# A hybrid decoder layer whose input projection is regrouped by one level of Strassen's algorithm in two passes

## The chip, the cores and the metric

The kernel runs on one core of one Trainium2 chip. A core has five engines that run at the same time, each with an instruction queue of its own that it works through strictly in order: TensorE (PE in the profile) multiplies matrices and writes its sums to PSUM, VectorE (DVE), ScalarE (ACT) and GpSimd (POOL) work element by element, and SyncE (SP) here only issues DMAs between DRAM and the on-chip memory SBUF. Engines wait for each other through semaphores. PEld in the profile is the loading of TensorE's stationary operand, which runs beside the products.

The metric is the device time of one execution in microseconds (us); lower is better. Three runs of the kernel before gave 1719.65, 1719.75 and 1719.79 us, a median of 1719.75 us.

## The reference, cut to what matters

One decoder layer over 1024 positions and 2048 channels, all in float32:

```python
proj = x @ w_in                       # [1024, 2048] @ [2048, 7176]
q, k, v, g_att, fg, c_b, c_c, c_h, g_conv, p_u, g_pool = split(proj)
# 8 heads of 128: softmax of q k / sqrt(128) plus the forget gates' cumulative logs, causal
y_att  = forgetting_attention(q, k, v, fg, b_f) * silu(g_att)
y_conv = c_b * causal_conv3(c_c * c_h) * silu(g_conv)
y_pool = pool_map(causal_means(p_u)) * pool_scale * silu(g_pool)
x = layer_norm(2 ** 0.25 * x + concat(y_att, y_conv, y_pool) @ w_out)
```

Leaving out the eight forget logits `fg`, `proj` has 7168 columns: 56 blocks of 128. Eight of them are `v`, eight each are `q`, `k` and `g_att`, and 24 belong to the convolution and the pooling.

## The kernel before

**Products.** [...] A matmul has a 128x128 stationary operand and up to 512 moving columns.

**Stages.** `x`, transposed, is loaded once (`load_x`), split, and kept on chip as 32 tiles of [128, 2, 512]. First come `v` and the forget logits, with positions on partitions: `x` is the stationary operand, and the weights move in chunks of 512, 260 and 260 columns (`V_CHUNKS`); the results go to `v_dram`. Then 48 blocks of 128 columns are projected in the transposed layout (`project`, `run_project`): the weights are stationary, and `x` moves in two halves of 512 positions. A block takes 16 (parts of the 2048 channels) x 2 (halves) x 3 = 96 matmuls. The last stage multiplies the gated branches `y`, which are reloaded from `y_dram`, with `w_out` and ends in the LayerNorm.

**What sets the order.** Weights come through a stream: `w_load` issues the DMA on SP, `w_split` splits, and `next_w` keeps two splits and two loads ahead. The work of a branch is written as a list of steps; `run_project` takes one step of `side` (gates, attention) and one of `pooling` after every 12 matmuls. The 24 steps of a head's attention (`attention_steps`) so run under the 288 matmuls of the next head's three blocks. A scheduler then orders each engine's queue at build time, by its own model of when an operand will be there; that order is fixed on the chip.

**Attention of a head.** `scores` computes a block of 128 keys by 512 queries and adds the gate term on DVE; `fold` keeps the running maximum on DVE. `across` and `to_all` bring the row values to all partitions by way of `m_dram`. `probs` adds them to the scores (DVE, line 392), takes the exponential (ACT), folds the sum (POOL, line 361) and splits the result (ACT, DVE). `values` multiplies with `v`, `finish` applies the gate and stores `y`. Pooling's window sums (`means`) run on POOL.

```python
def mm3(acc, wh, wl, xh, xl, start, stop):
    nc.tensor.matmul(acc, wh, xh, start=start, stop=False)
    nc.tensor.matmul(acc, wh, xl, start=False, stop=False)
    nc.tensor.matmul(acc, wl, xh, start=False, stop=stop)
```

Of the kernel before, what the change touches and what calls it, by code (L numbers as in the profile page):

```python
# [26 lines left out]
P = 128  # L27
# [6 lines left out]
V_CHUNKS = (512, 260, 260)  # L34
# [5 lines left out]
SLOTS = 46  # L40
WARM_UP = 8


@with_exitstack
def layer(ctx: ExitStack, tc: tile.TileContext, xt, x, wm, wv, b_f, conv_w, pool_w, pool_scale,
# [3 lines left out]
    sb = ctx.enter_context(tc.tile_pool(name="sb", bufs=1))  # L49
# [9 lines left out]
    # one float32 [128, 1024] row block  # L59
    def f4(name):  # L60
        return sb.tile([P, S], F32, tag="b", bufs=SLOTS, name=nm(name))

    # high and low part of a [128, 512] block
    def hl(name):
        return sb.tile([P, 2, H], F32R, tag="b", bufs=SLOTS, name=nm(name))

# [7 lines left out]
    def mm3(acc, wh, wl, xh, xl, start, stop):  # L74
        nc.tensor.matmul(acc, wh, xh, start=start, stop=False)  # L75
        nc.tensor.matmul(acc, wh, xl, start=False, stop=False)  # L76
        nc.tensor.matmul(acc, wl, xh, start=False, stop=stop)  # L77

    # ---- constants
# [15 lines left out]
    # the tensor engine's clock comes up while the first loads are under way  # L95
# [8 lines left out]
    v_dram = dr.tile([NST, P, D // 2], F32, tag="vd", name="v_dram")  # L104
    y_dram = dr.tile([KT, 2, P, H], F32, tag="yd", name="y_dram")
    c_dram = dr.tile([NH * NST, P], F32, tag="cd", name="c_dram")
    m_dram = dr.tile([NH * 4, H], F32, tag="md", name="m_dram")

    # ---- weights: a stream of [128, <=512] chunks, split as they arrive
# [3 lines left out]
    def w_load(src, cols):  # L113
        raw = sb.tile([P, 512], F32, tag="wr", bufs=4, name=nm("wr"))
        nc.sync.dma_start(raw[:, :cols], src)
        return raw, cols

    def w_split(raw, cols):
        hi = sb.tile([P, 512], F32R, tag="wh", bufs=3, name=nm("wh"))
        lo = sb.tile([P, 512], F32R, tag="wl", bufs=3, name=nm("wl"))  # L120
        split(hi[:, :cols], lo[:, :cols], raw[:, :cols])
        return hi, lo

    plan = deque()
    v0 = 0
    for w in V_CHUNKS:
        for k in range(KT):
            plan.append((wv[k, :, v0 : v0 + w], w))
        v0 += w
    n_mt = wm.shape[0]  # L130
    for m in range(n_mt):
        for kc in range(4):
            plan.append((wm[m, kc], 512))
# [14 lines left out]
    xs = [[hl("x"), hl("x")] for _ in range(KT)]  # L148
    fgz = const.tile([P, NST, NH], F32, tag="fgz", name="fgz")

    def load_x(k):
        raw = f4("xraw")
        for h in range(2):
            cuts = [0, 128, 512] if k == 0 and h == 0 else [0, 512]
            for c0, c1 in zip(cuts, cuts[1:]):
                cs = slice(h * H + c0, h * H + c1)
                nc.sync.dma_start(raw[:, cs], xt[k, :, cs])
                if k == 0 and h == 0 and c0 == 0:
                    fill()
                split(xs[k][h][:, 0, c0:c1], xs[k][h][:, 1, c0:c1], raw[:, cs])  # L160

    v0 = 0
    for c, w in enumerate(V_CHUNKS):
        banks = [bank("acc") for _ in range(4)] + [bank("aux") for _ in range(4)]
        for k in range(KT):
            if c == 0:
                load_x(k)
                if k == 2:
                    nc.sync.dma_start(bf_sb, b_f.partition_broadcast(P))
                    nc.sync.dma_start(cw_sb, conv_w)  # L170
                    nc.sync.dma_start(psc_sb, pool_scale)
            wh, wl = next_w()
            for st in range(NST):
                sl = slice(st % 4 * P, st % 4 * P + P)
                xk = xs[k][st // 4]
                mm3(banks[st][:, :w], xk[:, 0, sl], xk[:, 1, sl], wh[:, :w], wl[:, :w], k == 0, k == KT - 1)
        cols = min(w, D // 2 - v0)
        for st in range(NST):
            vf = f4("vf")
            if st % 2:  # L180
# [515 lines left out]
```

## Time and profile before

| what | value |
|---|---|
| runs (3) | 1719.65 to 1719.79 us, median 1719.75 |
| the profiled execution: its span | 1719.5 us |
| around the span, by the median of the runs | 0.25 us |
| VectorE, ScalarE, GpSimd busy in the whole span | 46%, 27%, 9% |
| weight chunks loaded for `proj`, transposed layout | 192 of 256 KB, 2.7 us to landing |
| mean DMA rate over the span | 91 GB/s |
| written to DRAM in the span | 19.50 MB |

The page gives no time of the profiled execution but its span, from the first to the last instruction. A share of busy time is an average over stages: VectorE's 46% hides that its tenths in the page's 40 slices run at 6 to 7 during attention and at 1 to 3 in the projections of pooling and convolution. The chain that ended last is followed back from the last instruction, and tells which engine's work could not be moved without moving the end.

### The profile page before, as it was taken

The page shows a single profiled execution, that of the slowest core. Times are in us where ns is not written, and L with a number is a line of the kernel's source. Part 1 is how long each engine was busy: PE and PEld are TensorE (multiplying, and loading weights), DVE is VectorE, ACT ScalarE, POOL GpSimd, SP SyncE. Part 2 cuts the span into 40 slices and gives each one's busy share as a digit, 9 for nine tenths or more (in the row PEclk, how much of TensorE's full clock was granted, in tenths as well). Part 3 has the DMA queues.
Part 4 walks back from the last instruction along what each step waited for, and adds up shares of the span by engine and source line. Part 5 has one row for each costly group of instructions (what it writes and reads, how often), then busy time and mean ns, then how long its engine had stood idle before and what let it go on. Part 6 is the DMA issues. An engine that isn't in the chain of part 4 may idle for free.

```text
span 1719.5 us, 20754 instructions
## 1 busy us (share of the span) xinstructions
PE 1698.1 (99%) x7965; PEld 1420.8 (83%) x7965; DVE 792.7 (46%) x1486; ACT 470.0 (27%) x857; POOL 154.3 (9%) x204
## 2 busy tenths in 40 slices
PE   9999999999999999999999999999999999999997
PEld 7899888888888888888878888888888888887686
DVE  4221326676767676766751212121213443365436
ACT  4211223342433333433421111111112332232210
POOL 0000000211212020202132230000000000000000
PEclk9999999999999999999999999999999999999999
DMA  6232322222222222212222121211112554355523
GB/s 223 90 114 75 88 61 60 82 68 82 66 74 68 82 73 68 92 54 89 68 76 63 56 61 49 62 49 50 47 47 65 185 188 140 120 171 178 173 69 101
DMA packets 95043, 155.94 MB, mean 91 GB/s; under 512 B 11168, under 2 KB 26592, under 8 KB 94944
## 3 DMA queue, kind: packets, MB, share of 16 engines
q1 hardware_dynamic: 94944, 154.62, 29.9%
q8 instruction: 62, 1.02, 0.3%
q14 instruction: 37, 0.30, 0.1%
HBM read 135.08 MB, written 19.50 MB: 90 GB/s over the span
## 4 chain that ended last, share of the span: by engine, by line
PE 89%; DMA 5%; DVE 3%; issue 1%; ACT 1%; POOL 1%; SPq 0%; DVEq 0%
PE acc L75 24%; PE acc L76 24%; PE acc L77 24%; PE aux L76 6%; PE aux L77 5%; PE aux L75 5%; DMA wr<-w_out 4%; DVE wl L72 1%; ACT wlast L71 1%; DMA m<-m_dram 0%; DVE r L595 0%; DVE pt L72 0%; DVE r L596 0%; DVE bst L565 0%; DVE t L392 0%
## 5 line engine op out<-in xcount | busy, mean ns | idle before, releaser
L75 PE MATMUL acc<-x,wh 128*128 128x512 f32 x1536 | 598.8, 390 | 0.0
L76 PE MATMUL acc<-x,wh 128*128 128x512 f32 x1536 | 598.1, 389 | 0.0
L77 PE MATMUL acc<-x,wl 128*128 128x512 f32 x1536 | 597.9, 389 | 0.0
L72 DVE TENSOR_TENSOR wl<-wr,wh 128x512 fp32r<-128x512 f32 (+1 forms) x352 | 243.4, 694 | 588.8 <-ACT wh L71 583.9
L71 ACT CAST wh<-wr 128x512 fp32r<-128x512 f32 (+1 forms) x352 | 210.2, 602 | 778.4 <-PE acc L76 524.4
L77 PEld LDWEIGHTS acc<-x,wl 128*128 128x128 f32 x1536 | 288.4, 188 | 60.9
L75 PEld LDWEIGHTS acc<-x,wh 128*128 128x128 f32 x1536 | 288.6, 188 | 57.7
L76 PEld LDWEIGHTS acc<-x,wh 128*128 128x128 f32 x1536 | 288.6, 188 | 57.3
L76 PE MATMUL acc<-wl,y 128*128 128x512 f32 x256 | 100.4, 392 | 2.5 <-DVE wl L72 2.3
L75 PE MATMUL acc<-wh,y 128*128 128x512 f32 x256 | 100.0, 390 | 0.1
L77 PE MATMUL acc<-wh,y 128*128 128x512 f32 x256 | 99.7, 390 | 0.0
L76 PE MATMUL aux<-wl,y 128*128 128x512 f32 x192 | 75.8, 395 | 2.3 <-DVE wl L72 2.3
L75 PE MATMUL aux<-wh,y 128*128 128x512 f32 x192 | 75.6, 394 | 1.9 <-ACT wh L71 1.9
L361 POOL TENSOR_TENSOR m<-m,t 128x256 f32<-128x256 f32 (+1 forms) x64 | 74.7, 1168 | 23.8 <-ACT t L393 19.9
L77 PE MATMUL aux<-wh,y 128*128 128x512 f32 x192 | 75.3, 392 | 0.0
L72 DVE TENSOR_TENSOR pt<-t,pt 128x512 fp32r<-128x512 f32 (+1 forms) x96 | 71.8, 763 | 4.5 <-ACT pt L71 2.9
L392 DVE TENSOR_TENSOR t<-t,m 128x512 f32<-128x512 f32 (+1 forms) x96 | 58.5, 658 | 25.6 <-DMA m<-m_dram 25.2
L71 ACT CAST pt<-t 128x512 fp32r<-128x512 f32 (+1 forms) x96 | 49.9, 530 | 73.7 <-DVE pt L72 61.6
L351 DVE SCALAR_TENSOR_TENSOR t<-aux,t 128x512 f32<-128x512 f32 (+1 forms) x96 | 52.5, 547 | 30.9 <-PE aux L77 29.8
L593 POOL TENSOR_TENSOR r<-r,gb 128x512 f32<-128x512 f32 x1 | 1.7, 1673 | 697.6 <-ACT r L592 697.6
L75 PE MATMUL acc<-wh,x 128*128 128x260 f32 (+1 forms) x192 | 61.3, 319 | 0.0
L76 PE MATMUL acc<-wl,x 128*128 128x260 f32 (+1 forms) x192 | 61.0, 318 | 0.1
(152 smaller groups left out, 1899.0 us busy)
## 6 DMA issues: line engine op xcount, KB each, us to landing
wr<-wm SPq DMA_DIRECT2D x192, 256.0 KB, 2.7
wr<-w_out SPq DMA_DIRECT2D x128, 256.0 KB, 3.4
m<-m_dram SPq DMA_DIRECT2D x32, 256.0 KB, 3.6
out<-r SPq DMA_DIRECT2D x32, 256.0 KB, 2.8
xraw<-xt SPq DMA_DIRECT2D x31, 256.0 KB, 4.3
xr<-x SPq DMA_DIRECT2D x31, 256.0 KB, 4.0
yraw<-y_dram SPq DMA_DIRECT2D x26, 256.0 KB, 3.7
y_dram<-gate SPq DMA_DIRECT2D x24, 256.0 KB, 2.0
```

Source lines behind the costliest of these rows:

```text
L71: nc.scalar.copy(hi, src)
L72: nc.vector.tensor_tensor(lo, src, hi.bitcast(F32), ALU.subtract)
L75: nc.tensor.matmul(acc, wh, xh, start=start, stop=False)
L76: nc.tensor.matmul(acc, wh, xl, start=False, stop=False)
L77: nc.tensor.matmul(acc, wl, xh, start=False, stop=stop)
L351: nc.vector.scalar_tensor_tensor(tj[:, c0:H], acc[:, c0:], SCALE, tj[:, c0:H], ALU.mult, ALU.add)
L361: eng.tensor_tensor(m[:, c0:H], prev[:, c0:H], t[n, j][:, c0:H], op)
L392: nc.vector.tensor_tensor(tj[:, c0:H], tj[:, c0:H], mx[n][:, H + c0 :], ALU.add)
L593: nc.gpsimd.tensor_tensor(r, r, gb[1][:, cs], ALU.mult)
```

## The change

**The algorithm.** Two 128-column blocks of `w_in` form a pair (28 pairs). For a pair, `proj` is a 2x2 block product: two halves of the positions by two halves of the channels on one side, two halves of the channels by two blocks of columns on the other. Strassen's algorithm (in Winograd's form) makes such a product from 7 block products instead of 8, by sums and differences of blocks taken before and after. A block product is 8 x 3 = 24 matmuls of 512 columns (`Pair.product`).

**Two passes.** The first pass goes over all pairs and does four products of each (`p1`, `p6`, `p5`, `p7`), with the operands `11`, `s1`, `s2`, `s3` of `x` (`s` are sums). POOL makes the three weight combinations (`mix`, `mix_last`) from four raw blocks of 512 KB, and DVE and ACT split them as [128, 1024] tiles (`operand`). Two partial results of 512 KB per pair and one weight combination go to DRAM (`a_dram`, `b_dram`, `t_dram`). The second pass does the other three products (`12`, `22`, `s4`) with weights from the stream, and adds each to its partial result, which is loaded back (`load_pair`, `second`). Attention, pooling and convolution run beside the second pass; `tick` takes a step after every third channel part, that is after 9 matmuls.

**Other parts.** `v` is a pair's block like the others, in the transposed layout, and is turned by 8 transposes of 128x128 per head on TensorE (`turn_v`). The forget logits take 64 matmuls of their own, with the 16 columns of high and low parts stationary (`gate_sums`). The addition in `probs` and two multiplications of the convolution are on POOL. All of `y` goes through DRAM. The on-chip tiles lie in three pools that follow one another (first pass; second pass; output projection), so that a pool's first tiles reuse memory of the pool before.

```diff
+    def load_22(k):
+        row, r22 = rows[k], half("x22", "xr")
+        nc.sync.dma_start(r22, xt[KH + k, :, H:])
+        s1 = row[:, H:]
+        nc.vector.tensor_tensor(s1, s1, r22, ALU.add)
+        nc.gpsimd.tensor_tensor(r22, s1, row[:, :H], ALU.subtract)
+        nc.sync.dma_start(s2_dram[k], r22)
+        keep_x("s2", k, r22)
+        keep_x("s1", k, s1)
...
+        def mix(self):
+            r = self.raw
+            self.t3 = f4("t3", "w1")
+            nc.gpsimd.tensor_tensor(self.t3, r[3], r[1], ALU.subtract)
+            nc.gpsimd.tensor_tensor(r[1], r[1], r[0], ALU.subtract)
+            nc.gpsimd.tensor_tensor(r[3], r[3], r[1], ALU.subtract)
+
+        def mix_last(self):
+            r = self.raw
+            nc.gpsimd.tensor_tensor(r[2], r[2], r[3], ALU.subtract)
+            nc.sync.dma_start(t_dram[self.p], r[2])
+
+        def product(self, acc, src, name, more=False):
+            wh, wl = operand(src)
+            for k in range(KH):
+                ws = slice(k * P, k * P + P)
+                x = xs[name, k]
+                mm3(acc, wh[:, ws], wl[:, ws], x[:, 0], x[:, 1], not more and k == 0, k == KH - 1,
+                    skip_group_check=more)
...
+        def p6(self):
+            self.b, self.u2 = bank("aux"), half("u2", "u2")
+            self.product(self.b, self.raw[3], "s2")
+            nc.vector.tensor_tensor(self.u2, self.b, self.ca[:, :H], ALU.add)
...
+    for p in pairs[2:-2]:
+        p.load(0, 1, 3, 2)
+        p.mix()
+        p.mix_last()
+        p.p1()
+        p.p6()
+        p.p5()
+        p.p7()
...
+    def second(p, j):
+        acc, name = bank("acc"), LATER[j][0]
+        for c in range(2):
+            wh, wl = next_w()
+            for i in range(4):
+                k = c * 4 + i
+                ws = slice(i * P, i * P + P)
+                x = xs[name, k]
+                mm3(acc, wh[:, ws], wl[:, ws], x[:, 0], x[:, 1], k == 0, k == KH - 1)
+                tick()
+        ca, cb = arrived[p]
+        dst = (ca[:, :H], ca[:, H:], cb[:, :H])[j]
+        nc.vector.tensor_tensor(dst, acc, dst, ALU.add)
...
+        def turn_v(n):
+            def go():
+                acc, th = bank("aux"), hl("v", "v")
+                for a in range(4):
+                    c = (n * 4 + a) * P
+                    nc.tensor.transpose(acc[:, a * P : a * P + P], vt[:, c : c + P], ident)
+                split(th[:, 0], th[:, 1], acc)
+                v[n] = th
+            return go
...
         def probs(n, j):
             def go():
                 tj, c0 = t[n, j], first(n, j)
                 cw = min(c0, 256)
-                nc.vector.tensor_tensor(tj[:, c0:H], tj[:, c0:H], mx[n][:, H + c0 :], ALU.add)
+                nc.gpsimd.tensor_tensor(tj[:, c0:H], tj[:, c0:H], mx[n][:, H + c0 :], ALU.add)
                 nc.scalar.activation(tj[:, c0:H], tj[:, c0:H], AF.Exp)
```

**How the order moves.** Three places matter to what follows. In the prints below a name's number only tells tiles apart.

POOL, the second half of the queries of one head's attention. Before, its only two-tensor work there was the running sum `m`:

```order
L370 MEMSET w_626_4376 32x32
L361 TENSOR_TENSOR m_3697<-t_3698 128x512
L361 TENSOR_TENSOR m_3697<-m_3697,t_3759 128x512 x2
L361 TENSOR_TENSOR m_3697<-m_3697,t_3814 128x512
L361 TENSOR_TENSOR m_3697<-m_3697,t_3814 128x384
L361 TENSOR_TENSOR m_3697<-m_3697,t_3884 128x256
```

The same place in the change (line 639 is the addition in `probs`, line 608 the sum):

```order
L639 TENSOR_TENSOR t_4863<-t_4863,m_4862 128x512 x2
L639 TENSOR_TENSOR t_4922<-t_4922,m_4862 128x512 x2
L639 TENSOR_TENSOR t_4972<-t_4972,m_4862 128x512
L639 TENSOR_TENSOR t_4972<-t_4972,m_4862 128x384
L639 TENSOR_TENSOR t_5056<-t_5056,m_4862 128x256
L639 TENSOR_TENSOR t_5056<-t_5056,m_4862 128x128
L608 TENSOR_TENSOR m_4862<-t_4863 128x512
L608 TENSOR_TENSOR m_4862<-m_4862,t_4922 128x512 x2
```

Eight additions now stand on POOL ahead of the eight folds, and the exponentials, splits and `values` products wait for them.

DVE, one pair of the first pass in the change (`wop` is the low part of a product's weights; `u`, `ca`, `cb` are results taken out of PSUM):

```order
L277 TENSOR_TENSOR u_131_822<-aux_821,ca_791 128x512
L110 TENSOR_TENSOR wop_932<-wb_915,wop_931 128x1024
L282 TENSOR_TENSOR cb_853<-acc_852,u_131_822 128x512
L110 TENSOR_TENSOR wop_963<-wb_919,wop_962 128x1024
L286 TENSOR_TENSOR ca_791<-aux_821,ca_791 128x512
L287 TENSOR_TENSOR cb_853<-acc_852,ca_791 128x512
L110 TENSOR_TENSOR wop_994<-wb_917,wop_993 128x1024
L110 TENSOR_TENSOR wop_1023<-t_144_923,wop_1022 128x1024
```

The splits of the next pair's weights (`wop_932` and on) have moved ahead of this pair's last evacuations, so that a product's operands stand ready a product early.

SP where the output projection begins. Before, the loads of `y` stand among the loads of `w_out`, the first four of them far earlier, and no store stands there:

```order
L115 DMA wr_10303<-w_out 128x512
L115 DMA wr_10343<-w_out 128x512
L286 DMA yraw_10297<-y_dram 128x512
L286 DMA yraw_10320<-y_dram 128x512
L115 DMA wr_10383<-w_out 128x512
```

In the change:

```order
L156 DMA wr_10359<-w_out 128x512
L156 DMA wr_10381<-w_out 128x512
L530 DMA y_dram<-pa_9828 128x512 x2
L538 DMA yraw_10282<-y_dram 128x512
L538 DMA yraw_10284<-y_dram 128x512
L538 DMA yraw_10286<-y_dram 128x512
```

The first load of `y` now stands behind the store of the last convolution block's `y`.

SP between the two passes of the change (there is no such place before); `ca` and `cb` are the last pairs' partial results:

```order
L291 DMA a_dram<-ca_4033 128x1024
L292 DMA b_dram<-cb_4237 128x1024
L482 DMA pa_4408<-a_dram 128x1024
L483 DMA pb_4409<-b_dram 128x1024
L482 DMA pa_4412<-a_dram 128x1024
L483 DMA pb_4413<-b_dram 128x1024
L156 DMA wr_4417<-wp 128x512
```

The second pass's first weights `wr` stand behind the last stores and four loads of 512 KB.

More of the change, by code (lines that the diff above doesn't have):

```diff
@@ L162, in layer @@
[L162 to L177, printed above, removed]
[L178 to L187 removed]
+    xs = {}
@@ new lines, in layer @@
+    last_pairs = pairs[-2:]
+    for p in last_pairs:
+        p.load(0, 1, 3, 2)
+        p.mix()
+        p.mix_last()
+    for p in last_pairs:
+        p.p1()
+    for k in range(KH):
+        load_12(k)
+    for p in last_pairs:
+        p.p6()
+    for k in range(KH):
+        load_22b(k)
+    for p in last_pairs:
+        p.p5()
+    for k in range(KH):
+        load_s4(k)
+    for p in last_pairs:
+        p.p7()
+    leave()
+    enter("stream", STREAM)
+    small = enter("second", SECOND)
@@ L453, in means @@
             src, d, i = u, 1, 0
-            sums = [f4("sum"), f4("sum")]
+            sums = [f4("sum", "pl"), f4("sum", "pl")]
             while d < w:
```

460 lines of the change are left out of this document (294 added, 166 removed).

## The prediction, made before the change was timed

> **What bounds the kernel now.** I read the page first, for the engine that is never idle and for the chain that ended last, then the windows of three stages.
>
> ```profile
> span 1719.5 us, 20754 instructions
> ...
> PE 1698.1 (99%) x7965; PEld 1420.8 (83%) x7965; DVE 792.7 (46%) x1486; ACT 470.0 (27%) x857; POOL 154.3 (9%) x204
> ...
> PEclk9999999999999999999999999999999999999999
> ...
> PE 89%; DMA 5%; DVE 3%; issue 1%; ACT 1%; POOL 1%; SPq 0%; DVEq 0%
> ```
>
> PE is busy 99% of the span at full granted clock, and 89% of the chain is PE. That busy figure counts overlapping matmuls, so I take the price of a matmul from windows in which nothing else ran on PE: first the 260-column products for `v`, then a head's attention with the next head's blocks, then the last blocks of the projection (columns: busy time of PE, PEld, DVE, ACT, POOL, granted clock, DMA share, GB/s).
>
> ```profile
> 110.00:190.00 80.00, 80.00 (x653) 79.00 (x653) 19.16 (x52) 15.35 (x38) 2.02 (x9) 1.00 0.30 84
> ...
> 398.80:477.70 78.90, 78.90 (x362) 65.84 (x362) 54.44 (x112) 29.97 (x57) 12.89 (x17) 1.00 0.25 74
> ...
> 1120.00:1300.00 180.00, 180.00 (x796) 149.10 (x795) 39.10 (x53) 26.57 (x45) 0.00 (x0) 1.00 0.18 49
> ```
>
> A 512-column matmul costs 180.00 / 796 = 0.226 us, a 260-column one 80.00 / 653 = 0.1225 us. PE sets the time in every stage but the first and the last microseconds, so a matmul taken away is time taken away, as long as nothing else becomes late.
>
> **Term 1, the products: -135 us.** Before, 48 blocks of 96 matmuls are 4608 x 0.2261 = 1042 us; `v` takes 16 x 8 x 3 = 384 matmuls of 512 columns (87 us) and 768 of 260 (94 us): 1223 us. After, 28 pairs x 7 products x 24 = 4704 matmuls are 1064 us, and the gate sums' 64 are 14.5 us. The transposes are new; the nearest row is the one transpose of the gates.
>
> ```profile
> 200.82 0.39 PE L77 MATMUL acc<-x,wl 128*128 128x512 f32 x1
> 201.05 0.27 PE L227 MATMUL aux<-ident,cum 128*64 128x128 f32 x1
> 201.07 0.47 PE L75 MATMUL acc<-x,wh 128*128 128x512 f32 x1
> 201.39 0.39 PE L76 MATMUL acc<-x,wh 128*128 128x512 f32 x1
> ```
>
> From 200.82 to 201.39 run two 512-column products and the transpose: 0.57 - 0.45 = 0.12 us for it. Its 0.27 us of duration would be the upper end. At 0.12 us, 64 for `v` and 16 small ones take 10 us. 1064 + 14.5 + 10 = 1088, so 135 us go; at 0.27 us it would be 123.
>
> The Trainium skill (TensorE: Matmul & The Clock Gate, Part 4: PE-mode transpose) gives about 275 ns for a 128x128 transpose inside a kernel; by that the 80 would take 22 us and the sum would end 12 us later. The row's spacing speaks for the smaller price, but for one transpose only.
>
> **The first pass in steady state: nothing.** A pair's 96 matmuls last 21.7 us. Beside them stand the following.
>
> ```profile
> L72 DVE TENSOR_TENSOR wl<-wr,wh 128x512 fp32r<-128x512 f32 x320 | 229.6, 720 | 511.6 <-ACT wh L71 506.8 <-PE acc L76 4.7
> ...
> L421 DVE TENSOR_TENSOR gate<-aux,gate 128x512 f32<-128x512 f32 x16 | 10.6, 659 | 0.0
> ...
> L463 POOL TENSOR_TENSOR sum<-sum,u 128x1024 f32<-128x1024 f32 x4 | 10.0, 2504 | 0.3
> ...
> 5.00:10.00 5.00, 4.83 (x20) 3.54 (x20) 2.79 (x5) 2.21 (x4) 0.00 (x0) 1.00 0.88 290
> ```
>
> POOL's four combinations take 4 x 2.5 = 10 us. DVE's four splits of 1024 columns (2 x 0.72 each) and four evacuations (0.66) take 8.4 us. Seven transfers of 512 KB are 3.7 MB, which at the 290 GB/s of the start are 12.7 us. All lie under 21.7 us, and the DVE rows of a pair show the next pair's splits ahead of this pair's evacuations. If that cover were gone, each us over 21.7 would cost 26 us, once per pair.
>
> **Term 2, the start: +22 us.** The first products now wait for 512 KB blocks, and by SP's order `p1` ends only when 7.1 MB have come: 7.1 MB / 290 GB/s + 3 = 27 us, while PE has 64 matmuls (14.5 us) for it. Then POOL is late: before the second half of `s2` it has 12 combinations of 2.5 us, four of them for the third pair, and 8 subtractions of 512 columns.
>
> ```profile
> 4.60 0.60 PE L75 MATMUL acc<-wh,x 128*128 128x512 f32 x1
> ...
> L361 POOL TENSOR_TENSOR m<-m,t 128x512 f32<-128x512 f32 x24 | 38.1, 1589 | 20.6 <-ACT t L393 19.9
> ...
> xraw<-xt SPq DMA_DIRECT2D x31, 256.0 KB, 4.3
> ```
>
> 12 x 2.5 + 8 x 1.59 = 43 us from about 13 us on (3.2 MB stand on SP up to the first pair's third block), and some 10 us (two such loads in a row) for `x` blocks whose buffers come free only after a store: 66 us. `p6`'s rest and two `p5` products follow (13 us), which makes 79 us for 224 matmuls (51 us): 28 us idle. Before, the first product starts at 4.6 us, and 20 matmuls instead of 22 in the window from 5 to 10 us show what little is lost later: about 6 us in all. The difference is 22. Bounds: +5 if DMA alone counts, +35 if POOL and loads never overlap.
>
> **Term 3, two handovers: +14 us.**
>
> ```profile
> wr<-wm SPq DMA_DIRECT2D x192, 256.0 KB, 2.7
> ...
> yraw<-y_dram SPq DMA_DIRECT2D x26, 256.0 KB, 3.7
> y_dram<-gate SPq DMA_DIRECT2D x24, 256.0 KB, 2.0
> ...
> cq<-c_dram SPq DMA_DIRECT2D x8, 512.0 KB, 4.0
> ```
>
> Between the passes SP holds the first `wr` loads behind the stores of the last results: two evacuations (1.3), a store of 512 KB (about 3, from 2.0 for half), the `pa` and `pb` loads and the weights (4.0), the cast (0.6): some 10 us, of which 16 gate products cover 3.6. At the output projection the first `y` load stands behind the last `y` store: evacuation and product (0.66 + 1.4), load (3.7), cast and split (1.3): 7 us. Together 14; bounds 6 (loads go ahead) and 24 (each waits for a full landing in turn).
>
> **Term 4, attention: +40 us.** Steps now come after 9 matmuls instead of 12, so PE would need 78.9 - 72 x 0.226 + 8 x 0.12 = 63.6 us per head. DVE's 54.4 us change by -12 additions in `probs`, +6 splits of 0.72, +9 accumulations of 0.66 and about 4 instructions of pooling or convolution of 0.72:
>
> ```profile
> L392 DVE TENSOR_TENSOR t<-t,m 128x512 f32<-128x512 f32 (+1 forms) x96 | 58.5, 658 | 25.6 <-DMA m<-m_dram 25.2
> ...
> L361 POOL TENSOR_TENSOR m<-m,t 128x256 f32<-128x256 f32 (+1 forms) x64 | 74.7, 1168 | 23.8 <-ACT t L393 19.9
> ```
>
> 54.4 - 7.9 + 4.3 + 5.9 + 2.9 = 59.6 us. POOL's 12.9 us grow by 12 x 1.17 and by 2.5 (convolution) to 9 (pooling): 29 to 36 us. And the two engines get in each other's way:
>
> ```profile
> 386.11 3.07 POOL L361 TENSOR_TENSOR m<-m,t 128x512 f32<-128x512 f32 x2 [0.33 <-ACT t L393]
> ...
> 386.25 1.78 DVE L72 TENSOR_TENSOR pt<-t,pt 128x512 fp32r<-128x512 f32 x1
> 387.95 1.77 DVE L72 TENSOR_TENSOR wl<-wr,wh 128x512 fp32r<-128x512 f32 x1
> 389.65 0.68 DVE L72 TENSOR_TENSOR pt<-t,pt 128x512 fp32r<-128x512 f32 x1
> ...
> 392.26 1.38 DVE L392 TENSOR_TENSOR t<-t,m 128x128 f32<-128x128 f32 x1
> ...
> 394.17 1.50 DVE L72 TENSOR_TENSOR pt<-t,pt 128x512 fp32r<-128x512 f32 x1
> ```
>
> A DVE subtraction takes 0.68 us alone and 1.78 beside a POOL fold. The four lengthened ones here lose about 4 us to 12.9 us of POOL work, 0.32 us per us; 16 to 23 us more of POOL work so add 5 to 7 us. DVE comes to 65 to 67 us per head against PE's 64: from 69% busy to full. I take 69 us per head, DVE's load and a few waits in order: +5 x 8 = +40. Bounds: 0, if every wait disappears under PE; +14 a head, if half of the 24.5 us that DVE sat idle in the window before stay.
>
> The Trainium skill (SBUF — State Buffer, Who interferes with whom) says that a DVE instruction with two SBUF inputs and a GpSimd instruction that reads SBUF exclude each other for a whole instruction. The rows agree (1.78 against 0.68 us), and it speaks against moving `probs`' addition to POOL: by it alone, with no overlap left between POOL's 33 us and DVE's 60, a head would take 93 us and the kernel 1856. The second rival below is this mechanism, priced by rows.
>
> **The sum.** The profiled execution's span is 1719.5 us, 0.25 under the median of the runs. 1719.5 - 135 + 22 + 14 + 40 = 1660.5, and 1661 us with what lies around it.
>
> **The rivals.**
> - PE stays the bound in attention too: term 4 is nothing, 1621 us. For it: DVE's waits for ACT in the page are waits for free buffers, not work that is late. Against it: 65 us of DVE in 64.
> - DVE and POOL set attention's pace: at 78 us a head, some +112, 1733 us. Place: `probs`' additions and folds in line on POOL, the weight splits behind them on DVE. It decides the sign from (135 - 36) / 8 = 12.4 us above 63.6, that is 76 us a head. For it: the lengthened rows. Against it: the exclusion took only 4 us per head so far.
> - The first pass is not bound by PE, since POOL, stores and loads wait for each other in SP's single queue: at 23.2 us a pair, +39, 1700 us. Against it: 12.7 us is the longest load beside 21.7. That fewer products are not had at all is ruled out by the order: 4704 matmuls stand there.
>
> **How the numbers follow.** The forecast, 1661 us, has a chance of 0.62; with the bounds of terms 2 and 3 and a head between 65 and 73 us it spans 1625 to 1700. PE bound throughout 0.20; DVE and POOL 0.12, three quarters of it slower; the first pass 0.06. The range is 1612 to 1722. About 0.2% is what a measurement of this kernel can tell from no change: faster by more than that 0.88, within it 0.03, slower 0.09.
>
> **What would show it.** Of the terms: the windows of the first pass should show 96 matmuls in 21.7 us per pair; PE should wait some 28 us in the first 80 us, for POOL's subtractions last; two gaps of 6 to 8 us should stand where the passes change; a head should take 66 to 73 us with DVE above 90%. The prediction is wrong if PE waits in the first pass, or if a head takes under 65 or over 74 us.

## The result and the profile after

The changed kernel takes 1832.4 us, the median of four runs (1830.65 to 1834.0); the kernel before took 1719.7 beside it. The ratio is 1.066 (95% interval 1.064 to 1.067): **slower by 112.7 us**, where 59 us less were forecast, and outside the range of 1612 to 1722.

The page of the changed kernel, in the same lines as before:

```profile
span 1831.5 us, 19913 instructions
...
PE 1645.2 (90%) x7053; PEld 1327.4 (72%) x7053; DVE 1081.2 (59%) x1643; ACT 581.9 (32%) x919; POOL 612.2 (33%) x436
...
PEclk7799999999999997989899989999998999999999
...
PE 55%; DVE 13%; DMA 12%; POOL 12%; issue 6%; ACT 2%; SPq 0%; DVEq 0%; POOLq 0%; ACTq 0%
```

PE has 912 instructions fewer and is no longer the whole of the chain: DVE, DMA and POOL hold 37% of it. The row of the clock is new: it was 9 in all 40 slices before. The two stages at the kernel's beginning are seen in the windows of both kernels (busy time of PE, PEld, DVE, ACT, POOL, granted clock, DMA share, GB/s), first after, then before:

```profile
0.00:100.00 100.00, 73.77 (x260) 51.69 (x261) 74.08 (x72) 34.34 (x51) 56.06 (x50) 0.80 0.61 216
100.00:600.00 500.00, 500.00 (x2207) 414.02 (x2206) 222.41 (x182) 108.47 (x115) 240.70 (x90) 1.00 0.46 160
600.00:720.00 120.00, 91.68 (x369) 69.55 (x368) 45.95 (x61) 30.00 (x46) 30.29 (x18) 0.87 0.59 203
```

```profile
0.00:100.00 100.00, 98.72 (x459) 82.43 (x460) 37.03 (x61) 34.96 (x60) 2.15 (x29) 1.00 0.52 165
```

From 100 to 600 us the first pass runs as forecast, 500 us for 2207 products, 0.2266 us each, at full clock and without a wait. At the start and around 680 us PE loses what it lost nowhere before. The third place is attention. The next two windows run from the first score product of head 0 to that of head 7, so they hold seven heads; before, then after:

```profile
252.88:805.40 552.52, 552.20 (x2521) 459.90 (x2520) 379.15 (x775) 208.59 (x390) 90.72 (x119) 1.00 0.25 74
```

```profile
745.10:1339.90 594.80, 500.09 (x2098) 398.86 (x2098) 446.60 (x824) 259.95 (x453) 239.40 (x238) 0.92 0.36 120
```

A head took 552.5 / 7 = 78.9 us with 360 products; it takes 594.8 / 7 = **85.0 us with 300**. DVE is busy for 63.8 us of it and POOL for 34.2: neither is full, and PE waits.

What each stage lost, from the spacing of PE's successive products in the timeline less what they take at full rate (0.2266 us per 512 columns), as the difference from the kernel before:

| stage | forecast, us | measured, us | of it at half clock |
|---|---|---|---|
| products fewer, by their count and the spacing measured | -135 | -135 | |
| start, 0 to 100 us | +22 | +42 | 9 |
| first pass in steady state | 0 | -2 | |
| handover between the passes, 600 to 720 us | +7 | +37 | 5 |
| attention, 720 to 1450 us | +40 | +171 | 42 |
| handover to the output projection and rest | +7 | +4 | -1 |

The sum is +117 beside a span that is 112 us longer; the 5 us between are small irregularities of spacing that I did not follow. The last column depends on where a gap is taken to end and a slow product to begin, and is good to about 10 us.

**What waits in attention.** From the list of waits of the changed kernel (who waited for whom, us in total, times, the longest):

```profile
ACT t L640 <- POOL t L639: 95.1, 61, 10.4
ACT pt L109 <- PE aux L115: 83.3, 39, 8.2
...
PE aux L114 <- DVE pt L110: 65.2, 33, 7.2
...
DVE m L618 <- POOL m L608: 34.4, 8, 6.3
```

PE's wait for a split of `pt` on DVE is the last link (a split is ACT's cast of a value to its high part and DVE's subtraction, which leaves the low part). How it comes about shows in the timeline of one head, for POOL, DVE and PE (start, duration, in brackets the idle time before it and who ended it):

```profile
886.22 9.63 POOL L639 TENSOR_TENSOR t<-t,m 128x512 f32<-128x512 f32 x8 [4.28 <-DMA m<-m_dram]
895.82 1.72 POOL L608 TENSOR_TENSOR m<-t 128x512 f32<-128x512 f32 x1
897.62 7.06 POOL L608 TENSOR_TENSOR m<-m,t 128x512 f32<-128x512 f32 x6
```

```profile
898.01 1.78 DVE L110 TENSOR_TENSOR wh<-wr,wh 128x512 fp32r<-128x512 f32 x1
904.71 0.71 DVE L618 STREAM_TRANSPOSE m<-m 128x512 f32<-128x512 f32 x1 [4.92 <-POOL m L608]
905.35 0.65 DVE L110 TENSOR_TENSOR pt<-t,pt 128x512 fp32r<-128x512 f32 x1
```

```profile
899.96 0.40 PE L113 MATMUL acc<-x,wh 128*128 128x512 f32 x1
906.05 0.79 PE L114 MATMUL aux<-pt,v 128*128 128x512 f32 x1 [5.69 <-DVE pt L110]
906.64 0.63 PE L115 MATMUL aux<-pt,v 128*128 128x512 f32 x1
907.07 0.63 PE L114 MATMUL acc<-x,wh 128*128 128x512 f32 x1
```

POOL does eight additions and seven folds in one line, 18.5 us. DVE has nothing to do for 4.92 us, but its next instruction in order is the reduction of the folded sums (L618), and the split that PE needs stands behind it, as does the next weight split. PE loses 5.7 us, and then its products start 0.43 us apart in place of 0.2266.

### The profile page after: what moved, and what is told of

Read it like the earlier page. It is cut to its first block, busy times and chain, and to the rows that moved or that the text cites. A ratio compares the mean times of both kernels' runs of the same rounds, so it can differ in the third digit from the quotient of the medians.

```text
span 1831.5 us, 19913 instructions
## 1 busy us (share of the span) xinstructions
PE 1645.2 (90%) x7053; PEld 1327.4 (72%) x7053; DVE 1081.2 (59%) x1643; ACT 581.9 (32%) x919; POOL 612.2 (33%) x436
## 4 chain that ended last, share of the span: by engine, by line
PE 55%; DVE 13%; DMA 12%; POOL 12%; issue 6%; ACT 2%; SPq 0%; DVEq 0%; POOLq 0%; ACTq 0%
PE acc L114 11%; PE acc L113 11%; PE acc L115 11%; PE aux L114 7%; PE aux L115 7%; PE aux L113 7%; DMA wr<-w_out 3%; POOL t L639 3%; POOL m L608 3%; DVE wh L110 2%; DMA m<-m_dram 2%; DMA wb<-wp 1%; DVE pt L110 1%; DVE x L110 1%; POOL sum L695 1%
## 5 line engine op out<-in xcount | busy, mean ns | idle before, releaser
L113 PE MATMUL acc<-x,wh 128*128 128x512 f32 x672 | 275.8, 410 | 18.3 <-ACT wh L109 18.3
L110 DVE TENSOR_TENSOR wh<-wr,wh 128x512 fp32r<-128x512 f32 x280 | 208.2, 747 | 131.5 <-ACT wh L109 130.9
L109 ACT CAST wh<-wr 128x512 fp32r<-128x512 f32 x280 | 171.9, 619 | 332.5 <-PE acc L115 236.7
L114 PE MATMUL acc<-x,wh 128*128 128x512 f32 x672 | 273.8, 408 | 0.0
L115 PE MATMUL acc<-x,wh 128*128 128x512 f32 x672 | 272.7, 406 | 1.3 <-DVE wh L110 1.3
L109 ACT CAST wop<-wb 128x1024 fp32r<-128x1024 f32 x84 | 88.4, 1053 | 318.4 <-PE aux L114 158.7
L113 PE MATMUL acc<-x,wop 128*128 128x512 f32 x448 | 177.0, 397 | 10.2 <-ACT wop L109 8.5
L114 PE MATMUL acc<-x,wop 128*128 128x512 f32 x448 | 177.8, 397 | 6.2 <-DVE x L110 6.2
L115 PE MATMUL aux<-x,wop 128*128 128x512 f32 x448 | 176.9, 395 | 7.0 <-DVE wop L110 7.0
L114 PE MATMUL aux<-x,wop 128*128 128x512 f32 x448 | 176.9, 395 | 4.9 <-DVE x L110 4.9
L113 PE MATMUL aux<-x,wop 128*128 128x512 f32 x448 | 177.2, 396 | 3.0 <-ACT wop L109 1.9
L115 PE MATMUL acc<-x,wop 128*128 128x512 f32 x448 | 177.8, 397 | 1.1 <-DVE wop L110 1.1
L110 DVE TENSOR_TENSOR wop<-wb,wop 128x1024 fp32r<-128x1024 f32 x84 | 137.9, 1642 | 52.1 <-ACT wop L109 49.9
L113 PEld LDWEIGHTS acc<-x,wh 128*128 128x128 f32 x672 | 133.5, 199 | 44.4 <-ACT wh L109 18.9
L115 PEld LDWEIGHTS acc<-x,wh 128*128 128x128 f32 x672 | 133.0, 198 | 32.1 <-DVE wh L110 2.2
L114 PEld LDWEIGHTS acc<-x,wh 128*128 128x128 f32 x672 | 134.0, 199 | 25.4
L639 POOL TENSOR_TENSOR t<-t,m 128x512 f32<-128x512 f32 (+1 forms) x96 | 117.0, 1247 | 72.6 <-DMA m<-m_dram 72.6
L113 PE MATMUL acc<-wh,y 128*128 128x512 f32 x256 | 101.0, 394 | 8.5 <-ACT y L109 8.4
```

The costliest lines, as they stand in the source:

```text
L109: nc.scalar.copy(hi, src)
L110: nc.vector.tensor_tensor(lo, src, hi.bitcast(F32), ALU.subtract)
L113: nc.tensor.matmul(acc, wh, xh, start=start, stop=False, **more)
L114: nc.tensor.matmul(acc, wh, xl, start=False, stop=False, **more)
L115: nc.tensor.matmul(acc, wl, xh, start=False, stop=stop, **more)
L639: nc.gpsimd.tensor_tensor(tj[:, c0:H], tj[:, c0:H], mx[n][:, H + c0 :], ALU.add)
```

## The experiments

Each run is compared with the kernel before, run on the same chip beside it (1719.8 to 1720.4 us). "A head" is the mean of seven, taken as above.

**1. The addition of the maximum back on DVE.**

```diff
-                nc.gpsimd.tensor_tensor(tj[:, c0:H], tj[:, c0:H], mx[n][:, H + c0 :], ALU.add)
+                nc.vector.tensor_tensor(tj[:, c0:H], tj[:, c0:H], mx[n][:, H + c0 :], ALU.add)
```

> The changed kernel with one line changed: the addition of the maximum to the scores goes back from POOL to DVE. Theory A (POOL's line: additions and folds of a step need about 4.8 us on POOL against 2 us of matmuls, and DVE's reduction of the sums stands in order behind the folds, with the splits behind it): POOL's line is halved, the head goes from about 88 to about 78 us, 1740 to 1770 us. Theory B (DVE's load and the exclusion of DVE and POOL set the pace): DVE gets 12 x 0.68 = 8 us more per head, so no gain or a loss, 1825 to 1890 us.

1779.8 us (ratio 1.035, 1.033 to 1.037): 52.6 us less. The window of the seven heads:

```profile
744.80:1296.90 552.10, 485.45 (x2098) 390.17 (x2097) 478.79 (x908) 261.60 (x453) 144.99 (x154) 0.94 0.40 129
```

DVE has 4.6 us more per head (478.8 against 446.6 over seven), and a head still takes 6.1 us less, 78.9. So it is not DVE's load that held the head, but the waits for POOL. The gain falls 10 us short of the expected range: a head still takes 15 us more than the 63.6 of its products.

**2. The same addition on POOL in the kernel before.**

```diff
-                nc.vector.tensor_tensor(tj[:, c0:H], tj[:, c0:H], mx[n][:, H + c0 :], ALU.add)
+                nc.gpsimd.tensor_tensor(tj[:, c0:H], tj[:, c0:H], mx[n][:, H + c0 :], ALU.add)
```

> The kernel before with the same addition on POOL, as in the changed kernel, and nothing else. Theory A: a step of the second half has two additions and two folds, 4.8 us of POOL against 12 matmuls = 2.7 us, over four steps up to 8 us of waiting per head, of which the empty steps take some: 1745 to 1785 us. Theory B: DVE is 69% busy per head and loses 8 us of its own load, so nothing is late: 1717 to 1727 us.

1766.2 us (1.026, 1.025 to 1.028), 46.3 us slower, by this line alone, and inside theory A's range.

```profile
252.50:844.00 591.50, 567.52 (x2521) 468.93 (x2520) 352.29 (x693) 212.18 (x394) 186.12 (x203) 0.97 0.23 69
```

DVE is *less* busy than before (50.3 us per head against 54.2), POOL is at 26.6 of 84.5 us, and the kernel is slower: what counts is who waits for POOL, not a load. The two runs price the move of this addition from both sides, 46 and 53 us.

**3. and 4. Without the window sums, and then with four `pt` buffers.**

```diff
-            src, d, i = u, 1, 0
-            sums = [f4("sum", "pl"), f4("sum", "pl")]
...
-            nc.gpsimd.tensor_tensor(env["z"], src, u, ALU.subtract)
+            env["z"] = u
```

```diff
-SECOND = {..., "pl": (4, 2), "cq": (4, 1), "t": (4, 7), "pt": (4, 2)}
+SECOND = {..., "cq": (4, 1), "t": (4, 7), "pt": (4, 4)}
```

> The changed kernel without the pooling window sums (left out: the means over the windows and the subtraction, z is u itself), which stand on POOL in heads 0 to 3. Theory A: heads 0 to 3 stop losing more than heads 4 to 7, about 8 us per 100 us of them: 25 to 45 us less, 1790 to 1810 us. Theory B: only the lengthening of DVE's subtractions by 5 to 10 us of POOL work per head goes, 0.32 us per us: 6 to 12 us less, about 1822 us.

> As the run without the window sums (left out the same), and the room of their tiles goes to the pt tiles: four buffers in place of two. Theory C (two pt buffers hold ACT, and with it everything behind, until the products have read them: 83 us of ACT waiting in 39 places): 30 to 60 us under the run without the window sums. Theory A: ACT only waits for products that are themselves late, and POOL's line stays, under 12 us.

1802.4 us without the sums (30 us less than the changed kernel), 1775.7 with four buffers (26.7 us less again). The first is inside theory A's range. The second lies between the two theories: two buffers do hold ACT, and with it the line, but for less than the 83 us of its waits suggest; that many of these hide behind other waits is likely, but was not shown.

**5. and 6. The handover and the start, one edit each.**

```diff
-    for k in range(KH):
-        load_s4(k)
     for p in last_pairs:
         p.p7()
...
+            fill()
             load_pair(0)
             load_pair(1)
             for j in range(3):
                 for q in range(2):
                     second(q, j)
+                    if j < 2:
+                        load_s4(4 * j + 2 * q)
+                        load_s4(4 * j + 2 * q + 1)
```

```diff
     for p in pairs[2:-2]:
         p.load(0, 1, 3, 2)
-        p.mix()
-        p.mix_last()
+        with tc.issue_after(late["sub"].ins):
+            p.mix()
+            p.mix_last()
```

(`late["sub"]` is the last of POOL's subtractions for `s2`; the combinations are queued behind it.)

> The changed kernel with s4 put together after the first second-pass products (which use x12 and x22 only) in place of before them, its loads in the wr buffers, and the first two weight loads ahead of the parked blocks' loads. Theory D (the 18.5 us gap at 682 us comes from SP's order: s4's loads through four buffers, then two stores and four loads of 512 KB, stand before the first weight load): the gap falls to 5 to 8 us, and the rest of the wait before it shrinks, 1815 to 1822 us. Rival: the pools that follow one another hold the weight buffers until the last product of the first pass is done, and s4 is only moved into attention's start: within 4 us of 1832.

In the changed kernel, SP stands behind `s4`'s loads, stores and the loads of the parked blocks, and issues the first weight load only at 694.67 us (SP's timeline):

```profile
685.01 0.33 SPq L225 DMA_DIRECT2D s2b<-s_dram  x1
...
688.40 0.32 SPq L291 DMA_DIRECT2D a_dram<-ca  x1
...
694.30 0.32 SPq L483 DMA_DIRECT2D pb<-b_dram  x1
694.67 1.97 SPq L156 DMA_DIRECT2D wr<-wp  x4
```

PE's gap there, in the changed kernel and in the run with `s4` later:

```profile
682.24 0.40 PE L323 MATMUL aux<-x,fw 128*16 128x512 f32 x1
700.96 0.80 PE L113 MATMUL acc<-x,wh 128*128 128x512 f32 x1 [18.33 <-ACT wh L109]
```

```profile
679.39 0.40 PE L323 MATMUL aux<-x,fw 128*16 128x512 f32 x1
683.15 0.79 PE L113 MATMUL acc<-x,wh 128*128 128x512 f32 x1 [3.36 <-ACT wh L109]
```

The gap falls from 18.5 to 3.5 us, more than was expected, yet the median is 1828.1 us, 4.3 us less, and the single runs (1823.0 to 1832.6) overlap with those of the changed kernel (1830.65 to 1834.0). From 600 to 720 us PE loses 12 us less, since other waits there grow, and 7 come back from 720 to 800 us, where `s4`'s splits now stand among attention's first steps (gaps and half clock 19 us there against 12). That SP's order makes the gap is shown, though the edit moves `s4`'s loads and brings the first weight loads forward at once and does not tell the two apart; most of the gain is given back, and the time is nearly the rival's.

> The changed kernel with POOL's four combinations of the third pair queued behind the eight subtractions for s2 in place of between them. Theory E (POOL is late at the start): the last subtraction comes up to 10 us earlier, 8 to 12 us less, about 1822 us. Rival (DVE, 100% busy for 20 to 30 and 65 to 80 us, and the loads that wait for buffers decide there; or the third pair then comes late in its turn): within 3 us of 1832.

1827.1 us, 5.4 us less: the right direction, half of the size.

**7. Filling the gap.**

```diff
+            spare = bank("aux")
+            for _ in range(80):
+                nc.tensor.matmul(spare, xs["12", 0][:, 0, :P], xs["12", 0][:, 0], start=True, stop=True)
             load_pair(0)
```

> The changed kernel with 80 additional products of 512 columns (80 x 0.2266 = 18.1 us; their result is used nowhere) on PE in the 18.5 us gap before the second pass. Theory F (a gap halves the clock for some microseconds after it: 16 products took 6.1 us there in place of 3.6): the first products of the second pass run at 0.2266 us, and the time falls by 2 to 4 us although PE does more, 1828 to 1830 us. Rival (the slow products come from the loads and splits of the second pass's start, not from the clock): the spacing after the gap stays at 0.4 us and the time at 1832 or above.

1838.1 us, 5.7 us more. The products ran from 678.84 to 697.1 us, the weights came no sooner, and a gap of 3.7 us was left. The windows around it:

```profile
695.00:698.00 3.00, 2.14 (x10) 1.44 (x8) 0.00 (x0) 0.00 (x0) 0.00 (x0) 1.00 1.01 396
698.00:700.00 2.00, 0.00 (x0) 0.00 (x0) 0.00 (x0) 0.00 (x0) 0.00 (x0) 1.00 1.01 384
700.00:702.00 2.00, 1.16 (x3) 0.93 (x4) 1.18 (x2) 1.70 (x3) 0.00 (x0) 0.53 1.06 415
702.00:705.00 3.00, 3.00 (x9) 2.12 (x8) 0.88 (x2) 0.15 (x1) 0.00 (x0) 0.50 0.72 283
```

As a test of a saving it failed, since the gap was not closed. It shows something else: 3.7 us without a product halve the clock for as long (6.1 us, from 700.84 to 706.97) as the 18.5 us of the changed kernel did. Most of the added time is the 16 gate products of the second pass: in the changed kernel they end ahead of the gap (the row at 682.24 above), here they stand behind the filling, from 704.85 to 709.50 us, and take 4.65 us of the second pass. The first of them are slow too, although they need nothing from the stream of weights, and the granted clock is 0.50 there: that speaks for the clock and against the rival.

**8. and 9. The sums by TensorE, with the addition on DVE and on POOL.** Two products with ones per block of keys replace POOL's folds, DVE's reduction and the way through DRAM.

```diff
-                if j:
-                    fold(n, j, ALU.add, nc.gpsimd)
...
+                nc.tensor.matmul(sm[n][:, cw:], ones_r, th[:, 0, cw:], start=j == 0, stop=False)
+                nc.tensor.matmul(sm[n][:, cw:], ones_r, th[:, 1, cw:], start=False, stop=j == 4 * n + 3)
...
-                w = across(n, ALU.add)
-                nc.vector.reciprocal(w[:, :16], w[:, :16])
-                to_all(n, w, h * 4 + 2 + n)
+                nc.vector.reciprocal(mx[n][:, H:], sm[n])
```

> The changed kernel with the addition back on DVE and the sums of the probabilities taken by TensorE (two products with ones per block of keys, 24 more per head, 4.6 us) in place of POOL's folds, DVE's reduction and the round trip through DRAM. POOL then has nothing of attention. Theory A (what is late is POOL's line and DVE in order behind it): the 99 us of attention's gaps and 33 us of half clock of the run with the addition on DVE fall below a third; 1779.8 + 37 - 90 = about 1727, 1710 to 1745 us. Theory C (two pt buffers and DVE's own order are what is left): the gaps of 4 to 5 us per head before the products with pt stay; 1790 to 1815 us.

> The changed kernel with the sums of the probabilities on PE as in the run before this one, but with the addition of the maximum left on POOL. Theory A (additions and folds are one line on POOL, and taking away either half frees it): the line is 8 additions of 1.2 us per second half of a head against 8 us of matmuls; 37 us more of products and 50 to 70 us less waiting: 1795 to 1820 us. Rival (the folds, with DVE in order behind them, are the trouble, and the addition on POOL costs little): as the run with the addition on DVE, 1760 to 1775 us.

With the addition on DVE 1764.3 us (1.026, 1.024 to 1.027), 15.5 less than run 1 in spite of 37 us of added products; a head takes 76.2 us. Attention's losses fall to 76 us, not to a third of run 1's 132: theory A is right in kind and too large in size, and the time lies between the two ranges. With the addition on POOL 1819.5 us, 12.9 under the changed kernel, the upper edge of A's range: a head takes 83.6 us. So the folds alone do not explain the line, and the addition costs more (55 us between the two runs). In run 9 no reduction stands behind folds any more, so the addition has a price of its own; there too ACT's exponentials wait for POOL's additions.

```profile
ACT t L641 <- POOL t L640: 90.3, 60, 5.0
```

Both runs also pay for something that the edit brings: DVE now takes a reciprocal of 512 columns, some 3.35 us, twice a head, where the changed kernel has one of 16 columns (lines of the changed kernel and of run 8):

```profile
L661 DVE RECIPROCAL w<-w 32x16 f32<-32x16 f32 x16 | 3.7, 232 | 0.0
```

```profile
L661 DVE RECIPROCAL m<-acc 128x512 f32<-128x512 f32 x16 | 53.5, 3345 | 0.0
```

**10. to 12. Everything together.** Without the window sums, four `pt` buffers and the addition on DVE; then with the whole computation: addition on DVE, `s4` and third pair later, the window sums made in two halves of at most 528 columns so that a third `pt` buffer fits, and the row sums on PE or folded on POOL.

```diff
-SECOND = {..., "pl": (4, 2), "cq": (4, 1), "t": (4, 7), "pt": (4, 2)}
+SECOND = {..., "pl": (0, 2), "cq": (4, 1), "t": (4, 7), "pt": (4, 3)}
...
+            for n in (1, 0):
+                lead = 16 * n
+                src, d, i, size = u[:, n * H - lead : n * H + H], 1, 0, H + lead
```

> The run without the window sums and with four pt buffers (left out the same), and the addition on DVE. Theory G (three separate causes: POOL's additions, the window sums, the pt buffers): their gains add, 1775.7 - 53 = about 1723, 1715 to 1735 us, and attention loses under 50 us to gaps and half clock. Rival (with one of them gone another stands in its place, DVE at 90% of a head): 1745 to 1765 us.

> All that the runs showed so far, with the whole computation: addition on DVE, sums on PE, s4 put together later, third pair later, and the window sums made in two halves so that there is room for a third pt buffer. If the gains add: 1764 - 5 (third pair) - 4 (s4) - 15 to 25 (a third pt buffer): 1730 to 1742 us. If what is left is DVE beside the window sums and the loads of the maximum, the third buffer gives nothing: 1750 to 1758 us. Neither theory has it below the kernel before.

> The same without the sums on PE: POOL's folds stay, 37 us of products fewer. If the third pt buffer also loosens DVE's reduction behind the folds: 1779.8 - 5 - 4 - 25 = about 1745 us, level with the run with the sums on PE. If the folds keep their 50 us: 1755 to 1775 us.

1748.5, 1743.8 (1.014, 1.012 to 1.015) and 1758.5 us. In run 10 the gains do not add, and the time is in the rival's range: 27 us come from moving the addition where it was 53 alone, and DVE is at 88% of a head:

```profile
742.60:1263.70 521.10, 472.62 (x2098) 382.49 (x2098) 458.92 (x909) 259.78 (x453) 100.20 (x122) 0.96 0.42 137
```

Runs 11 and 12, with the whole computation, take back 89 and 74 of the 112.7 us; neither is faster than the kernel before, and no run was. Run 11 lies between its two ranges, run 12 in the range for folds that keep their price. In run 11 a head takes 74.5 us, of which 4.6 are the products with ones.

**13. POOL folds, and nobody waits in order behind them.** As run 12, with the folded sums split and multiplied with ones two steps later.

```diff
-                w = across(n, ALU.add)
-                nc.vector.reciprocal(w[:, :16], w[:, :16])
-                to_all(n, w, h * 4 + 2 + n)
+                th, acc = hl("sm", "pt"), bank("aux")
+                split(th[:, 0], th[:, 1], mx[n][:, :H])
+                nc.tensor.matmul(acc, ones_r, th[:, 0], start=True, stop=False)
+                nc.tensor.matmul(acc, ones_r, th[:, 1], start=False, stop=True)
+                nc.vector.reciprocal(mx[n][:, H:], acc)
...
```

> As the last run with POOL's folds, but no engine stands in order behind the folds any more: DVE's reduction and the round trip through DRAM are replaced by a split of the folded sums and two products with ones, two steps later (4 more products per head instead of 24). Theory A2 (a fold costs PE nothing by itself; what costs is DVE, and the splits queued on it, waiting in order behind the folds): attention loses as little as with all sums on PE, without its 37 us of products: 1743.8 - 37 + 7 = about 1714, 1705 to 1725 us. Theory A1 (the folds cost by lengthening DVE's instructions beside them): the gain is under half, 1735 to 1755 us.

1753.1 us (1.019, 1.017 to 1.021): only 5.4 less than run 12, and no head is faster for it (77.7 us against 76.9), so the gain lies outside the seven heads. The windows of run 12 and of run 13:

```profile
737.70:1276.10 538.40, 483.22 (x2097) 389.44 (x2096) 469.95 (x909) 259.48 (x456) 150.36 (x182) 0.94 0.41 132
```

```profile
733.10:1277.30 544.20, 499.27 (x2188) 400.30 (x2189) 506.48 (x819) 272.93 (x477) 162.88 (x169) 0.97 0.40 128
```

DVE is busy for 506.5 of 544.2 us, 93%, and now it is the pace. The time is in theory A1's range, but the run does not show theory A1, because this edit too brings the long reciprocal:

```profile
L669 DVE RECIPROCAL m<-aux 128x512 f32<-128x512 f32 x16 | 53.6, 3351 | 4.3 <-PE aux L668 4.3
```

In the seven heads these are 14 x 3.35 = 47 us of DVE, more than the 36.5 us by which DVE is busier than in run 12 (the reduction and its copies, which the edit takes out, go the other way). Instructions that both runs have, matched by tile and shape, take only some 9 us longer in run 13. So DVE is full mainly by what the edit gave it. Folds on POOL that nobody waits for, with a cheap reciprocal, were not run, and what they would cost stays open.

**14. Without POOL's combinations at the start.**

```diff
         def mix(self):
             r = self.raw
+            if self.p < 3:
+                self.t3 = r[3]
+                return
...
+            if self.p >= 3:
+                nc.gpsimd.tensor_tensor(r[2], r[2], r[3], ALU.subtract)
```

> The changed kernel without POOL's combinations of the first three pairs (left out: their products take blocks that are not combined). Theory E (the start is late by POOL's line and by DVE's splits that it lengthens): the 43 us that the start loses more than before fall by 15 to 30 us, 1803 to 1818 us. Rival (the loads, 7.1 MB before p1 ends and x blocks in buffers that come free late, decide): under 8 us, 1825 us or above.

1811.5 us, 20.9 less, inside theory E's range. PE is busy for 86.5 of the first 100 us in place of 73.8. So POOL's combinations make about half of what the start loses, by their own time on POOL or by lengthening DVE's splits; the run takes both away at once. Gaps and half clock are still some 29 us there, 24 more than before; whether loads or DVE's splits of `x` make these was not taken apart.

## Why the prediction was wrong

- **The products, and the first pass: right.** 2207 products in 500 us at full clock; POOL's 10 us, the stores and the loads all lay under them. The third rival (1700 us) fell.
- **The start: half the size, and another engine last.** 22 us were counted and 42 measured, 9 of them half clock, which was not counted. The sum had a line of POOL, and PE was to wait for POOL's subtractions last. In the trace the two longest late gaps end with DVE's splits, and POOL itself stood idle for 13.3 us before its first subtraction, waiting for an addition on DVE (changed kernel: PE, POOL, DVE, and the window from 65 to 85 us):

```profile
72.43 0.79 PE L114 MATMUL aux<-x,wop 128*128 128x512 f32 x1 [4.91 <-DVE x L110]
78.02 0.80 PE L115 MATMUL aux<-x,wop 128*128 128x512 f32 x1 [3.00 <-DVE wop L110]
```

```profile
47.58 7.55 POOL L207 TENSOR_TENSOR x<-xrow 128x512 f32<-128x512 f32 x4 [13.29 <-DVE xrow L206]
```

```profile
69.55 2.82 DVE L110 TENSOR_TENSOR x<-x,x 128x512 fp32r<-128x512 f32 x1
```

```profile
65.00:85.00 20.00, 10.99 (x29) 6.84 (x28) 19.54 (x15) 5.52 (x8) 13.33 (x6) 0.65 0.41 132
```

DVE is busy for 19.5 of these 20 us, and a split of 512 columns, 0.68 us alone, takes 1.8 to 2.8 us beside POOL. The sum had no term for DVE there.

- **The handovers: right in kind at the second, wrong at the first.** At the first the forecast put stores and loads in SP's line, but not the eight pairs of loads that build `s4` through four buffers, which stand ahead of them; and it did not look at the last two pairs, where PE waits too (4.5 us before 654.36 us, for ACT). Together 37 us in place of 7.
- **Attention: the step that failed** is "I take 69 us per head, DVE's load and a few waits in order". The load was sized well: DVE 63.8 us per head (65 to 67 forecast), POOL 34.2 (29 to 36 forecast). The waits were not: a head takes 21 us more than the 63.6 of its products, where 5 were forecast. A step of 9 products lasts 2 us, and in the second half of a head a step holds two additions and two folds, some 4.8 us of POOL. POOL therefore lags, by a line of 18 us in the head shown. ACT's exponentials wait for its additions (95 us in all), and DVE, with 25% to spare, stands in order behind its folds (34 us). The first wait does not need the second: run 9 has no fold on POOL and no reduction behind it, and the addition still costs 55 us. The sum of busy times could not show that; the order of the queues could have.
- **The second rival was the right one in its place**, POOL's additions and folds in line, with the splits behind them, which is what runs 1, 2, 8 and 9 bear out. Its price was 78 us a head, measured 85.0, and its chance of 0.12 was too low. "Against it: the exclusion took only 4 us per head so far" argued with a lightly used POOL. What it lacked are the two `pt` buffers (27 us by run 4) and the window sums (30 us by run 3): heads 0 to 3, beside which the window sums run, take 357.7 / 4 = 89.4 us, heads 4 to 6 79.0.

```profile
745.10:1102.80 357.70, 295.34 (x1210) 234.95 (x1209) 254.12 (x475) 153.57 (x267) 146.35 (x148) 0.90 0.35 116
1102.80:1339.90 237.10, 204.74 (x890) 163.90 (x889) 192.48 (x350) 106.39 (x187) 93.05 (x90) 0.96 0.38 125
```

- **A term that was missing: the clock.** Products that start more slowly after a gap cost some 54 us more than before (61 against 7), 42 of them in attention: about a fifth of the 252 us that the stages lost. The forecast priced every wait at its length alone. It was added up from spacings; no run took it away by itself.
- **The rule of the Trainium skill** (SBUF — State Buffer, Who interferes with whom) was right about the danger of moving the addition. Its reading as a sum, 93 us a head, came nearer than my 69, but in part by luck: DVE stood idle for 148 of the 594.8 us, waiting, and the sum has no place for that. How far DVE and POOL kept each other out cannot be read from their records, which together last 686 us in the 594.8, since a lengthened DVE instruction counts as busy all the while. The transposes, x64, have a mean duration of 272 ns, which agrees with the 275 that the Trainium skill (TensorE: Matmul & The Clock Gate, Part 4: PE-mode transpose) has, there for bf16; but a group of four takes 0.60 us in all, about 0.11 apart, so the smaller price was the right one.

```profile
853.68 0.60 PE L567 MATMUL aux<-ident,pa 128*128 128x128 f32 x4
```

Several causes overlap in attention: the addition on POOL (53 us), the window sums (30), the `pt` buffers (27) and the folds (56 of waiting between runs 1 and 8, of which the products with ones take back 37) together exceed what runs 10 and 11 gave. Part of that is the long reciprocal on DVE in runs 8 and 11. What one is worth depends on which others are left.

## What to carry to other kernels

Work taken from the bound engine is won only as long as each step's other engines finish within the shorter step: compare, step by step, the longest line of one engine (here 4.8 us of POOL) with the step's products (2 us), not the busy times over a stage. Before work is moved to an idle engine, look how much later its result comes there, and what stands in order behind that result on the engine that it leaves. Price what an edit puts in place of the work that it removes (here a reciprocal). And price each wait of the matrix engine at its length plus what the clock takes afterwards.

## What the runs showed of the hardware

**The clock after a gap.** In the changed kernel all eight gaps of PE over 5 us that were not followed at once by another were followed by products at half rate, for 4.95 us in the mean (6.1 at most), which costs 2.4 us each, whether the gap was 5 or 18.5 us long; of eight gaps of 3 to 5 us six were, and of 38 shorter ones 14, mostly where several stood close together. In the trace file of the changed kernel the granted clock changes in steps of 3.41 us: its stretches at half clock last 3.41, 6.83, 10.24 us and so on. The Trainium skill (TensorE: Matmul & The Clock Gate, Part 1) gives at least one window of about 3.4 us, idle to halve the clock and busy to restore it. The eight long gaps agree with it, and the half rate after them, 3.1 to 6.1 us, lies near one window or between one and two; the shorter gaps that half rate followed, some under 3 us, do not, taken singly.

**DVE beside POOL.** Runs 11 and 13 give DVE nearly the same instructions over seven heads (798 and 819; the 21 more in run 13, 14 of them splits, are some 14 us). With 69.5 us of POOL work beside it DVE is busy for 455 us, with 162.9 us for 506: (51 - 14) / 93 = 0.4 us per us of POOL, an estimate, where the forecast took 0.32 from a lightly loaded stretch. The window of run 11, beside that of run 13 above:

```profile
734.50:1255.80 521.30, 498.06 (x2267) 408.09 (x2268) 455.11 (x798) 262.31 (x456) 69.50 (x91) 0.98 0.41 131
```

**DVE's reciprocal.** For 128x512 it takes 3.34 to 3.35 us (runs 8, 9, 11 and 13; the line of run 13 is above), where a split of the same size takes 0.68 us alone.
